# Odd mixer of a diffusion trunk: queries go to the scores without their norm, and each row's 1/rms scales its exponential and its maximum

## Chip, cores and metric

One core of one Trainium2 chip runs the whole program in one launch. The metric is the device time in microseconds (us). The kernel before was run three times: median 2787.94, from 2787.29 to 2793.31.

## What is computed

One step of a two-layer trunk on 640 tokens (512 latent "sample" tokens and 128 "prompt" tokens): FFN, mixer, FFN in each layer. Layer 0 has the even mixer (windowed attention and an mLSTM), layer 1 the odd one (HGRN2 and a dense attention whose queries and keys are normed). The change lies in the attention of the odd mixer:

```python
def _rms(x, g, eps=1e-6):
    return x * lax.rsqrt(jnp.mean(x * x, -1, keepdims=True) + eps) * g

dq = _rms(dq.reshape(bsz, L, D_KV, D_HEADS // D_KV, HEAD_DIM), q_norm)   # 2 key heads x 4 query heads, 64 wide
dk = _rms(dk.reshape(bsz, L, D_KV, HEAD_DIM), k_norm)
...                                               # sample: axial rotary on dq, dk; prompt: none
s = jnp.einsum('bqhgd,bkhd->bhgqk', q, k) * (q.shape[-1] ** -0.5)
p = jax.nn.softmax(s, axis=-1)                    # no mask, no sink
y = jnp.einsum('bhgqk,bkhd->bqhgd', p, v)
```

The sample's queries see 640 keys (its own 512 and 128 cached ones), the prompt's queries see the prompt's 128 keys. The new keys and values of the prompt are outputs too.

## The kernel before

Everything is kept in fp32. Each large product is made of three passes over operands split into a high and a low part (`mm3`), so a projection of 128 columns costs 24 matmuls for each half of the tokens. The tokens lie in five chunks of 128; the halves are tokens 0 to 383 and 384 to 639 (`HALVES`, `CHUNKS`), and the prompt is the last chunk. The framework schedules the program as a whole: it writes a fixed order for the queue of each engine (PE is TensorE, DVE VectorE, ACT ScalarE, POOL GpSimd, SP SyncE), and each engine takes its queue strictly in that order.

`odd` (L1204) begins with `proj_group`: the keys, the values, the first 128 columns of queries (two heads) and the first column block of HGRN head 0 are projected for half 1 and then for half 2. Keys and queries go through `normed` (L1223). For one half its `ev` does this: ACT copies the projection from PSUM (`q<-pj`; for half 2 in two pieces, since the prompt's chunk is kept apart), ACT squares it (`qsq`), PE multiplies the squares by `hsel` to get the mean square of each token and head (`qss`), DVE adds eps (`qrs`), and POOL raises to the power -0.5 (`qrp`, L1239). Then `rest` follows: PE transposes the 1/rms so that tokens lie along the free axis (`qrt`), ACT copies that out of PSUM (`rr`), PE multiplies it by `bsel` so that each partition of a head holds it (`qrb`), DVE forms q times gain times 1/rms (`q<-q,oc,qrb`, L133), and `rope` turns the sample's tokens (two DVE and two POOL operations, L624 to L632).

`queries(g)` in `odd` brings the second 128 columns of the first key group (g = 0), and both 128-column blocks of the second (g = 1); so four query projections in all, eight halves, go through `normed`, besides the key's two.

`attention` (L806) is a generator. For each key group g it copies and splits the keys and queries (`att_keys`, `q_stack`: `att<-kT`, `att<-q`) and then takes five blocks of 128 queries: four of the sample with five key tiles each (640 keys), and one of the prompt (j = 4) with one key tile. For each block `att_probs` (L694) makes the scores of four heads in PSUM (`s`; 384 and 256 columns, two matmuls each), their row maxima on DVE (`mx`), minus the maximum (`nm<-mx`, `minus`), the exponentials on ACT with `nm` as bias and the row sums as a second result (`pq<-s,nm` and `E<-s,nm`), and multiplies by the reciprocal of the sums on DVE. `att_out` (L774) then transposes the probabilities on PE (`pT`), splits them (`pr`, ACT and DVE), and multiplies them by the values (`pv`).

`weave` (L878) runs the attention beside the projections of the HGRN heads (`projections`, with the matmuls `pj` and `pn`): between the steps of the one, steps of the other are put, and the scheduler then places these matmuls, here called fillers, between the attention's own. What fillers the attention does not use are left to the three HGRN heads that follow, which are woven with the rest of the same projections.

Of the kernel before, what the change touches and what calls it, by code (L numbers as in the profile page):

```python
# [8 lines left out]
F32 = mybir.dt.float32  # L9
# [3 lines left out]
AF = mybir.ActivationFunctionType  # L13
ALU = mybir.AluOpType
# [3 lines left out]
P = 128  # L18
# [5 lines left out]
HALVES = ((0, 384), (384, 640))  # L24
HMAX = 384
CHUNKS = ((0, 1, 2), (3, 4))
# [23 lines left out]
class Net:  # L50
# [53 lines left out]

    def sm(self, n, tag):
        return self.small.tile([P, n], F32, tag=tag, name=tag)

# [585 lines left out]

    def att_probs(self, q, ks, tiles, masks, nsink, room, out):  # L694


        nc = self.nc
# [6 lines left out]
        def minus(c):  # L704
            if nsink is None:
                self.ts(nm[:, c], mx[:, c], -1.0, ALU.mult)
            else:
                self.stt(nm[:, c], mx[:, c], -1.0, nsink[:, c], ALU.mult, ALU.min)

        two = []  # L710
        if len(tiles) == 1:
            p = self.bank("a2", "s1")
# [4 lines left out]
            for hd in range(4):  # L717
                r = room[hd][0][:, 0:P]
                self.act(r, p[:, hd * P:(hd + 1) * P], AF.Exp, bias=nm[:, hd:hd + 1], accum_out=su[:, hd:hd + 1])
                out.append([r])  # L720
            yield
        else:
            for hd in range(4):
# [26 lines left out]
                for n, (p, r) in enumerate(parts):  # L750
                    self.act(r, p, AF.Exp, bias=nm[:, c], accum_out=su[:, 4 * n + hd:4 * n + hd + 1])
                if len(parts) > 1:
# [12 lines left out]
        for hd in range(4):  # L765
            n = len(tiles)
# [36 lines left out]
    def attention(self, kT, vv, queries, spec, yds, room, nsink=None):  # L803

        ar = Arena(self.xpool.tile([P, self.XN], F32R, tag="x", name="att"))
        st = ar.take(4 * NT).rearrange("p (a b) -> p a b", a=4)  # L806
        kk = ar.take(2 * 768).rearrange("p (a b) -> p a b", a=2)
        pr = self.wp.tile([P, 2, 2, 512], F32R, tag="w", name="pr")
        pr = [(pr[:, n, 0], pr[:, n, 1]) for n in range(2)]
        ks = kk[:, 0], kk[:, 1]  # L810
        qs = yield from queries(0)
        for n in range(10):
            g, j = divmod(n, 5)
            if j == 0:
                self.att_keys(kk, kT, g)
                for b in range(2):
                    self.q_stack(st[:, 2 * b:2 * b + 2], qs[b])
            tiles, masks = spec[j]
            probs = []
            yield from self.att_probs(st[:, :, j * P:(j + 1) * P], ks, tiles, masks,  # L820
                                      None if nsink is None else nsink[:, 4 * g:4 * g + 4], room, probs)
            if n == 4:
                qs = yield from queries(1)
            self.att_out(g, j, tiles, probs, vv, pr, yds[g])
# [64 lines left out]
    def even(self, mod, tail):  # L889
# [45 lines left out]
        def queries(g):  # L935
            qs = [[self.ft(e - a, "q") for a, e in HALVES] for _ in range(2)]
            for n, q in enumerate(qs):
                yield from self.proj_steps(w, (2 * g + n) * P, ev_rope(q), "v")
            return qs

# [166 lines left out]
    def mlstm_head(self, h, ins, temps, yb, in_v, ma, col, tri):  # L1107
# [8 lines left out]
        for hf, ch in enumerate(CHUNKS):  # L1116
# [3 lines left out]
            self.act(kn[:, ch[0]:ch[-1] + 1], ps[:, :len(ch) * P].rearrange("p (c t) -> p c t", t=P))  # L1120
        ws = self.sm(10, "ws").rearrange("p (a b) -> p a b", a=2)

# [81 lines left out]
    def odd(self, mod, tail):  # L1204
# [17 lines left out]
        def normed(c0, dst, which, pool=None):  # L1222
# [3 lines left out]
            def ev(hf, p):  # L1226
# [8 lines left out]
                for n in range(len(ch)):  # L1235
                    self.mm(pv[:, 2 * n:2 * n + 2], sq[:, n * P:(n + 1) * P], hsel)
                rs, rp = self.sm(6, "qrs"), self.sm(6, "qrp")
                self.ts(rs[:, :nch], pv[:, 0:nch], 1e-6, ALU.add)
                nc.gpsimd.tensor_tensor(out=rp[:, :nch], in0=rs[:, :nch], in1=self.mhalf[:, 0:nch], op=ALU.pow)  # L1239

                def rest():
# [7 lines left out]
                    for s, e, o in segs[hf]:  # L1249
# [5 lines left out]
            return self.col_unit(w, c0, pool), ev  # L1255

        q0 = [self.ft(e - a, "q") for a, e in HALVES]
        ya0, ya1 = (self.yt((2, NT), F32, "hi") for _ in range(2))
# [3 lines left out]
        self.proj_group([normed(3072, kT, 1, "v"), (self.col_unit(w, 3200, "v"), lambda hf, p: self.act(vT[hf], p)),  # L1262
                         normed(2560, q0, 0, "v")] + [(self.col_unit(w, c0), ev) for c0, ev in ahead])
        self.out_rows(kT[1][:, 256:384], self.o["new_cache_d_k"][0, 0].rearrange("t g d -> t (g d)"))
# [3 lines left out]
        def queries(g):  # L1268
            qs = [q0] if g == 0 else []
            new = [[self.ft(e - a, "q") for a, e in HALVES] for _ in range(len(qs), 2)]  # L1270
            late = []
            for n, q in enumerate(new):
                (wh, wl), ev = normed(2560 + (2 - len(new) + 2 * g + n) * P, q, 0, "v")
                for hf, (a, b) in enumerate(HALVES):
                    p = self.bank(("a1", "b")[hf], "pj")
                    self.mm3(p[:, :b - a], [(wh[:, k], wl[:, k], self.hh[:, k, a:b], self.hl[:, k, a:b]) for k in range(KD)])
                    late.append(ev(hf, p[:, :b - a]))
                    yield
                    if len(late) > 1:
                        late.pop(0)()  # L1280
            late.pop(0)()
            return qs + new

# [298 lines left out]
```

## Time and profile before

| | |
|---|---|
| median of three runs | 2787.94 us |
| the profiled execution, own time | 2790.35 us |
| its span (first to last instruction) | 2788.5 us |
| mean granted TensorE clock | 0.984 |
| busy: PE, DVE, ACT, POOL | 96%, 64%, 34%, 9% of the span |

The profiled execution is 2.41 us above the median; its span is 1.85 us short of its own time. Times in the profile count from the start of the span. A granted clock of 1.00 is the 2.4 GHz level of TensorE, 0.50 the 1.2 GHz one. The odd mixer's projections begin at about 1850 us, its attention runs from about 1915 to 2110 us, and HGRN heads 0 to 3 follow.

### The profile page before, as it was taken

To read this page: it belongs to the slowest core of one execution; us is meant where nothing else is said; L and a number is where in the kernel's file an instruction comes from. 1 tells how busy PE (TensorE), PEld (TensorE's weight loads), DVE (VectorE), ACT (ScalarE), POOL (GpSimd) and SP (SyncE) were. 2 spreads that over 40 slices of the span, in tenths; PEclk is the share of its full clock that TensorE was granted. 3 is DMA by queue.
4 is the path that set the end of the run, shared out by engine and by line. 5 is a ranking of instruction groups with operands and counts; after the bars stand their busy time and mean duration, and the time that the engine had idled before them with its cause. 6 is when DMAs were issued, how large, how long until landed. Compare 5 with 4: busy or idle time off the path is not lost.

```text
span 2788.5 us, 46663 instructions
## 1 busy us (share of the span) xinstructions
PE 2685.5 (96%) x19101; PEld 2577.2 (92%) x19101; DVE 1780.5 (64%) x3477; ACT 948.0 (34%) x1944; POOL 247.8 (9%) x282
## 2 busy tenths in 40 slices
PE   7999999999999999999999999998999899999998
PEld 4999999899888999999999999987798789999997
DVE  4967864676767976533896783375677788333334
ACT  3321221555554421311422122144555435112122
POOL 1000000410013000000300000042100022000003
PEclk9999999999999999999999999998999999999999
DMA  7554532221122544422264452221012224223111
GB/s 244 175 151 117 167 119 84 71 73 48 40 73 77 171 132 128 133 66 68 69 181 129 118 170 80 58 85 50 16 46 67 71 78 144 61 69 99 55 60 54
DMA packets 308195, 271.56 MB, mean 97 GB/s; under 512 B 13947, under 2 KB 257421, under 8 KB 307981
## 3 DMA queue, kind: packets, MB, share of 16 engines
q1 hardware_dynamic: 307620, 268.44, 32.5%
q8 instruction: 150, 2.46, 0.4%
q14 instruction: 65, 0.52, 0.1%
q10 hardware_dynamic: 360, 0.14, 0.0%
HBM read 259.36 MB, written 9.18 MB: 96 GB/s over the span
## 4 chain that ended last, share of the span: by engine, by line
PE 76%; DVE 11%; DMA 6%; ACT 3%; issue 2%; POOL 1%; SPq 0%; POOLq 0%; DVEq 0%; ACTq 0%
PE ps L136 36%; PE po L136 22%; PE pj L136 7%; DMA rawa<-in_ada_w 3%; PE pn L136 3%; DVE acc L133 2%; DMA raw<-in_ffn_w 2%; DVE w L126 1%; PE pv L136 1%; PE pT L139 1%; PE s L136 1%; DVE x L133 1%; DVE sum L126 1%; DVE h L126 1%; DVE x L126 1%
## 5 line engine op out<-in xcount | busy, mean ns | idle before, releaser
L136 PE MATMUL ps<-h,w 128*128 128x256 f32 (+1 forms) x7584 | 1124.0, 309 | 5.3 <-DVE h L126 2.7
L136 PEld LDWEIGHTS ps<-h,w 128*128 128x128 f32 x7584 | 1116.7, 190 | 8.1 <-DVE h L126 3.5
L136 PE MATMUL po<-g,wv 128*128 128x256 f32 (+1 forms) x4224 | 633.4, 310 | 9.8 <-DVE x L133 6.0
L136 PEld LDWEIGHTS po<-g,wv 128*128 128x128 f32 x4224 | 622.7, 189 | 17.7 <-DVE x L133 6.9
L133 DVE SCALAR_TENSOR_TENSOR x<-po,mod,x 128x128 f32<-128x128 f32 (+1 forms) x576 | 236.0, 435 | 276.8 <-PE po L136 275.4
L126 DVE TENSOR_TENSOR w<-raw,w 128x1024 fp32r<-128x1024 f32 x208 | 254.5, 1228 | 123.0 <-ACT w L123 122.1
L133 DVE SCALAR_TENSOR_TENSOR acc<-rawa,sc,acc 128x512 f32<-128x512 f32 x448 | 319.8, 757 | 11.2 <-DMA rawa<-in_ada_w 10.7
L123 ACT ACTIVATE wv<-raw 128x1024 fp32r<-128x1024 f32 x120 | 124.4, 1056 | 577.7 <-PE po L136 457.3
L123 ACT ACTIVATE w<-raw 128x1024 fp32r<-128x1024 f32 x208 | 218.6, 1056 | 160.2 <-issue 81.3
L500 POOL TENSOR_TENSOR ssq<-ssq,sq 128x384 f32<-128x384 f32 (+1 forms) x84 | 84.8, 1009 | 1716.9 <-ACT sq L123 1716.4
L123 ACT ACTIVATE g<-gt 128x384 fp32r<-128x384 f32 (+1 forms) x176 | 82.1, 466 | 397.7 <-DVE gt L126 397.5
L126 DVE TENSOR_TENSOR wv<-raw,wv 128x1024 fp32r<-128x1024 f32 x120 | 147.1, 1231 | 105.7 <-ACT wv L123 105.5
L126 DVE TENSOR_TENSOR gt<-sl,ps 128x384 f32<-128x384 f32 (+1 forms) x176 | 85.3, 484 | 184.3 <-PE ps L136 183.9
L136 PE MATMUL pj<-h,w 128*128 128x384 f32 (+1 forms) x864 | 150.0, 317 | 0.5 <-ACT mi L123 0.5
L123 ACT ACTIVATE sl<-ps 128x384 f32<-128x384 f32 (+1 forms) x176 | 75.9, 432 | 203.7 <-PE ps L136 203.6
L136 PE MATMUL ps<-h,wv 128*128 128x256 f32 (+1 forms) x864 | 140.4, 314 | 4.2 <-ACT h L123 2.5
L136 PE MATMUL pn<-w,h 128*128 128x256 f32 x960 | 140.2, 289 | 1.3 <-ACT mi L123 0.9
L136 PEld LDWEIGHTS ps<-h,wv 128*128 128x128 f32 x864 | 129.2, 191 | 7.5 <-ACT h L123 3.6
L136 PEld LDWEIGHTS pj<-h,w 128*128 128x128 f32 x864 | 132.0, 192 | 3.5 <-issue 1.2
L136 PEld LDWEIGHTS pn<-w,h 128*128 128x128 f32 x960 | 124.8, 191 | 4.3 <-ACT mi L123 1.1
L136 PE MATMUL pj<-h,wv 128*128 128x256 f32 (+1 forms) x672 | 117.1, 323 | 3.8 <-DVE t L126 1.8
L136 PEld LDWEIGHTS pj<-h,wv 128*128 128x128 f32 x672 | 103.5, 197 | 7.2 <-issue 2.1
(327 smaller groups left out, 2493.3 us busy)
## 6 DMA issues: line engine op xcount, KB each, us to landing
raw<-in_ffn_w SPq DMA_DIRECT2D x264, 512.0 KB
rawa<-in_ada_w SPq DMA_DIRECT2D x144, 512.0 KB
raw<-in_w_in_odd SPq DMA_DIRECT2D x18, 512.0 KB
raw<-in_w_in_even SPq DMA_DIRECT2D x14, 512.0 KB
raw<-in_w_in_even SPq DMA_DIRECT2D x16, 256.0 KB
raw<-in_w_out_even SPq DMA_DIRECT2D x8, 512.0 KB
raw<-in_w_in_odd SPq DMA_DIRECT2D x16, 256.0 KB
raw<-in_w_out_odd SPq DMA_DIRECT2D x8, 512.0 KB
```

The costliest lines, as they stand in the source:

```text
L123: return self.nc.scalar.activation(out=out, in_=in_, func=func, **k)
L126: return self.nc.vector.tensor_tensor(out=out, in0=in0, in1=in1, op=op)
L133: return self.nc.vector.scalar_tensor_tensor(out=out, in0=in0, scalar=s, in1=in1, op0=op0, op1=op1)
L136: return self.nc.tensor.matmul(out=out, lhsT=lhsT, rhs=rhs, start=start, stop=stop)
L139: self.nc.tensor.transpose(out, in_, self.ident[:in_.shape[0], :in_.shape[0]])
L500: nc.gpsimd.tensor_tensor(out=sums[1], in0=sums[1], in1=sq, op=ALU.add)
```

## The change

The four query projections have a function of their own, `query`. ACT copies the projection with the gain as its scale (`q<-pj,oc`, one instruction for each half), and `rope` follows at once. The squares, the mean squares and the power are as before, but the power's result is written into a tile `rq` with one column for each chunk and head, with tokens along the partitions, and that is all of the norm: no `qrt`, `rr`, `qrb`, and no product on DVE. The scores come out as 1/rms short of what they were. `att_probs` gets `rs`, the four columns of the block: `minus` is now a `scalar_tensor_tensor` that forms minus the maximum times 1/rms, and the exponential takes a pointer to 1/rms as its scale. The keys are normed as before. The small tiles `ws`, `qrs`, `qrp` have two buffers where they had four, and `rq` has two. The even mixer passes no `rs`; its instructions and their order are those of before, and so are the FFNs'.

```diff
-    def att_probs(self, q, ks, tiles, masks, nsink, room, out):
+    def att_probs(self, q, ks, tiles, masks, nsink, room, out, rs=None):
...
         def minus(c):
-            if nsink is None:
+            if rs is not None:
+                self.stt(nm[:, c], mx[:, c], -1.0, rs[:, c], ALU.mult, ALU.mult)
+            elif nsink is None:
                 self.ts(nm[:, c], mx[:, c], -1.0, ALU.mult)
...
+        scale = lambda hd: 1.0 if rs is None else rs[:, hd:hd + 1]
...
                 for n, (p, r) in enumerate(parts):
-                    self.act(r, p, AF.Exp, bias=nm[:, c], accum_out=su[:, 4 * n + hd:4 * n + hd + 1])
+                    self.act(r, p, AF.Exp, bias=nm[:, c], scale=scale(hd), accum_out=su[:, 4 * n + hd:4 * n + hd + 1])
...
+        def query(c0, dst, rq, b):
+            def ev(hf, p):
+                a, ch = HALVES[hf][0], CHUNKS[hf]
+                nch = 2 * len(ch)
+                self.act(dst[hf], p, scale=gq[:, 0:1])
+                sq = self.ft(HALVES[hf][1] - a, "qsq")
+                self.act(sq, p, AF.Square)
+                pv = self.bank("a2", "qss")
+                for n in range(len(ch)):
+                    self.mm(pv[:, 2 * n:2 * n + 2], sq[:, n * P:(n + 1) * P], hsel)
+                rs = self.sm(6, "qrs", 2)
+                self.ts(rs[:, :nch], pv[:, 0:nch], 1e-6, ALU.add)
+                two = lambda t: t[:, :nch].rearrange("p (c h) -> p c h", h=2)
+                nc.gpsimd.tensor_tensor(out=rq[:, ch[0]:ch[-1] + 1, 2 * b:2 * b + 2], in0=two(rs), in1=two(self.mhalf), op=ALU.pow)
+                n = 384 if hf == 0 else P
+                self.rope(dst[hf][:, :n], dst[hf][:, :n], a, n)
+            return self.col_unit(w, c0, "v"), ev
...
-                         normed(2560, q0, 0, "v")] + [(self.col_unit(w, c0), ev) for c0, ev in ahead])
+                         query(2560, q0, rq0, 0)] + [(self.col_unit(w, c0), ev) for c0, ev in ahead])
```

The change moves instructions on TensorE's queue. A row of its order is line, operation, out<-in, shape and count; `pj` are fillers (projections for HGRN).

The first place is `proj_group` at the end of the keys' and the first queries' half 1 and in half 2, on PE. Before:

```order
L136 MATMUL qss<-oc,qsq 128x2 x3
L136 MATMUL pj<-h,wv 128x256 x4
L139 MATMUL qrt<-ident,qrp 2x128 x3
L136 MATMUL pj<-h,wv 128x256 x11
L136 MATMUL qrb<-rr,oc 128x384
L136 MATMUL pj<-h,wv 128x256 x22
L136 MATMUL qss<-oc,qsq 128x2 x2
L136 MATMUL pj<-h,wv 128x256 x6
L139 MATMUL qrt<-ident,qrp 2x128 x2
L136 MATMUL pj<-h,wv 128x256 x4
L136 MATMUL qrb<-rr,oc 128x256
L136 MATMUL pj<-h,wv 128x256 x6
```

With the change:

```order
L136 MATMUL qss<-oc,qsq 128x2 x3
L136 MATMUL pj<-h,wv 128x256 x36
L136 MATMUL qss<-oc,qsq 128x2 x2
L136 MATMUL pj<-h,wv 128x256 x4
L139 MATMUL qrt<-ident,qrp 2x128 x2
L136 MATMUL pj<-h,wv 128x256 x7
L136 MATMUL qrb<-rr,oc 128x256
L136 MATMUL pj<-h,wv 128x256 x6
L136 MATMUL pj<-h,w 128x256 x14
L136 MATMUL qss<-oc,qsq 128x2 x2
```

The transposes and broadcasts that are left are those of the keys' second half; the four of the queries are gone, and the two `qss` of half 2 have moved against them.

The second place is the start of the attention on PE: the last scores of the first block's heads 0 and 1, heads 2 and 3 (`s` in the rows after the fillers), the next block's first scores, and the first transposes `pT`. Before:

```order
L136 MATMUL s_18951<-att 128x384 x2
L136 MATMUL pj<-h,wv 128x384 x3
L136 MATMUL s_18963<-att 128x384 x2
L136 MATMUL pj<-h,wv 128x384 x12
L136 MATMUL pj<-h,wv 128x256 x24
L136 MATMUL s_19007<-att 128x384 x2
L136 MATMUL s_19011<-att 128x256 x2
L136 MATMUL s_19019<-att 128x384 x2
L136 MATMUL s_19023<-att 128x256 x2
L136 MATMUL s_19121<-att 128x384 x2
L136 MATMUL s_19133<-att 128x384 x2
L139 MATMUL pT<-ident,pq 128x128 x8
```

With the change:

```order
L136 MATMUL s_18926<-att 128x256 x2
L136 MATMUL pj<-h,wv 128x384 x24
L136 MATMUL s_18966<-att 128x384 x2
L136 MATMUL s_18970<-att 128x256 x2
L136 MATMUL pj<-h,wv 128x256 x3
L136 MATMUL s_18978<-att 128x384 x2
L136 MATMUL pj<-h,wv 128x256
L136 MATMUL s_18982<-att 128x256 x2
L136 MATMUL pj<-h,wv 128x256 x20
L136 MATMUL s_19080<-att 128x384 x2
L136 MATMUL s_19092<-att 128x384 x2
L139 MATMUL pT<-ident,pq 128x128 x8
```

Before, 36 fillers follow the scores of heads 0 and 1, and none lies between the scores of head 2 and the transposes. Now 24 follow them, and 24 more lie between the scores of heads 2 and 3 and behind them; the transposes are still eight in a row.

The third place is the prompt's block of the first key group on PE (`s` 128x128), at which `queries(1)` begins (`qss`). Before:

```order
L136 MATMUL s_19531<-att 128x384 x2
L136 MATMUL s_19535<-att 128x256 x2
L136 MATMUL pj<-h,w 128x384
L136 MATMUL s_19606<-att 128x128 x8
L136 MATMUL qss<-oc,qsq 128x2 x3
L139 MATMUL pT<-ident,pq 128x128 x8
L136 MATMUL pv<-pr,vals 128x512
L136 MATMUL pj<-h,w 128x256 x6
L136 MATMUL pv<-pr,vals 64x512
L136 MATMUL pv<-pr,vals 128x512
```

With the change:

```order
L136 MATMUL pj<-h,w 128x256 x2
L136 MATMUL s_19494<-att 128x256 x2
L136 MATMUL pj<-h,w 128x256 x4
L136 MATMUL s_19565<-att 128x128 x8
L136 MATMUL qss<-oc,qsq 128x2 x3
L136 MATMUL pj<-h,w 128x256 x17
L139 MATMUL pT<-ident,pq 128x128 x2
L136 MATMUL pj<-h,w 128x256
L139 MATMUL pT<-ident,pq 128x128 x6
L136 MATMUL pj<-h,w 128x384 x4
L136 MATMUL pv<-pr,vals 128x512
L136 MATMUL pj<-h,w 128x384 x7
```

Before, no filler lies between the squares' matmul `qss`, the transposes and the first `pv`; now there are 17, 1 and 4.

## Rows read from the trace of the kernel before

**Rows 1.** The page, busy time of each engine over the whole span: us (share of the span) x instructions.

```profile
PE 2685.5 (96%) x19101; PEld 2577.2 (92%) x19101; DVE 1780.5 (64%) x3477; ACT 948.0 (34%) x1944; POOL 247.8 (9%) x282
```

**Rows 2.** What TensorE waited for, 1850 to 2080 us (the odd mixer from its key projection to the second block of the second key group): us in total, times, longest.

```profile
PE qrt L139 <- POOL qrp L1239: 4.5, 3, 2.5
PE s L136 <- ACT pq L123: 3.7, 5, 1.5
PE pT L139 <- DVE pq L130: 2.8, 2, 1.4
```

**Rows 3.** Timeline of TensorE where the first two query halves and the key's second half are normed: start us, us, engine, line, operation, out<-in, count [idle before <- what released it].

```profile
1879.36 0.49 PE L139 MATMUL qrt<-ident,qrp 128*2 128x128 f32 x3 [1.20 <-POOL qrp L1239]
1879.61 1.55 PE L136 MATMUL pj<-h,wv 128*128 128x256 f32 x11
1881.09 0.91 PE L136 MATMUL qrb<-rr,oc 2*128 2x384 f32 x2
1881.93 2.90 PE L136 MATMUL pj<-h,wv 128*128 128x256 f32 x22
...
1888.67 0.58 PE L139 MATMUL qrt<-ident,qrp 128*2 128x128 f32 x2 [2.55 <-POOL qrp L1239]
...
1897.85 0.38 PE L139 MATMUL qrt<-ident,qrp 128*2 128x128 f32 x2 [0.73 <-POOL qrp L1239]
1898.06 0.27 PE L139 MATMUL pm<-ident,kT 128*128 128x128 f32 x1
...
1898.80 0.69 PE L136 MATMUL qrb<-rr,oc 2*128 2x256 f32 x2
1899.42 5.13 PE L136 MATMUL pj<-h,wv 128*128 128x384 f32 x28
```

**Rows 4.** Timeline of TensorE at the start of the attention, same columns.

```profile
1920.87 5.13 PE L136 MATMUL pj<-h,wv 128*128 128x384 f32 x36
1927.53 2.25 PE L136 MATMUL s<-att 128*128 128x384 f32 x8 [1.53 <-ACT pq L123]
1931.11 2.03 PE L136 MATMUL s<-att 128*128 128x384 f32 x4 [1.34 <-ACT pq L123]
1934.53 2.46 PE L139 MATMUL pT<-ident,pq 128*128 128x128 f32 x8 [1.39 <-DVE pq L130]
1937.47 1.84 PE L136 MATMUL pv<-pr,vals 128*128 128x512 f32 x3 [0.47 <-ACT pr L123]
```

**Rows 5.** Stretches: start:end, us, busy time of PE, PEld, DVE, ACT, POOL with counts, granted TensorE clock (1.00 is 2.4 GHz, 0.50 is 1.2 GHz), DMA share, GB/s.

```profile
1930.00:1942.00 12.00, 9.01 (x28) 5.75 (x29) 9.00 (x22) 6.24 (x14) 0.00 (x0) 0.50 0.04 11
1994.00:2000.00 6.00, 5.42 (x20) 3.76 (x19) 4.96 (x15) 2.80 (x10) 0.00 (x0) 0.50 0.00 0
2050.00:2060.00 10.00, 10.00 (x78) 9.62 (x77) 7.06 (x25) 5.38 (x20) 0.00 (x0) 1.00 0.00 0
2186.00:2204.00 18.00, 12.16 (x257) 10.23 (x252) 17.33 (x24) 9.81 (x17) 0.00 (x0) 1.00 0.16 43
```

**Rows 6.** Timeline of ScalarE at the first exponentials of the attention.

```profile
1925.51 1.28 ACT L123 ACT_TABLE_LOAD   x1 [1.85 <-DVE mx L126]
1926.80 0.58 ACT L123 ACTIVATE pq<-s,nm 128x384 f32<-128x384 f32 x1
```

**Rows 7.** Timeline of TensorE at the prompt's block (j=4) at the end of the first key group, at one query chain of the second pair, and at the prompt's block that ends the second key group.

```profile
1989.27 1.04 PE L136 MATMUL s<-att 128*128 128x128 f32 x8
1991.44 0.83 PE L136 MATMUL qss<-oc,qsq 128*128 128x2 f32 x6 [1.14 <-ACT pq L123]
1993.71 2.46 PE L139 MATMUL pT<-ident,pq 128*128 128x128 f32 x8 [1.44 <-DVE pq L130]
1996.71 0.79 PE L136 MATMUL pv<-pr,vals 128*128 128x512 f32 x1 [0.53 <-ACT pr L123]
...
2015.02 0.69 PE L136 MATMUL qrb<-rr,oc 2*128 2x256 f32 x2 [0.50 <-ACT rr L123]
...
2094.92 0.41 PE L139 MATMUL pT<-ident,pq 128*128 128x128 f32 x2 [0.94 <-DVE pq L130]
```

**Rows 8.** Groups of instructions, shapes apart, 1850 to 2110 us, on ScalarE, VectorE and GpSimd: line, engine, operation, out<-in, shapes, count | busy us, mean ns | idle before.

```profile
L123 ACT ACTIVATE pq<-s,nm 128x384 f32<-128x384 f32 x32 | 18.6, 581 | 12.5 <-DVE nm L130 12.2
L123 ACT ACTIVATE E<-s,nm 128x256 f32<-128x256 f32 x32 | 15.1, 471 | 0.1
...
L123 ACT ACTIVATE rr<-qrt 2x384 f32<-2x384 f32 x5 | 2.4, 473 | 4.8 <-PE qrt L139 4.8
...
L130 DVE TENSOR_SCALAR nm<-mx 128x1 f32<-128x1 f32 x32 | 4.8, 151 | 0.7
...
L133 DVE SCALAR_TENSOR_TENSOR q<-q,oc,qrb 128x384 f32<-128x384 f32 x4 | 2.5, 615 | 2.5 <-PE qrb L136 2.4
...
L1239 POOL TENSOR_TENSOR qrp<-qrs,mhalf 128x6 f32<-128x6 f32 x5 | 8.1, 1613 | 80.9 <-DVE su L764 70.6 <-DVE qrs L130 8.3 <-DVE var L126 1.9
```

**Rows 9.** The same view on ScalarE, 600 to 920 us (the even mixer): forms with and without a pointer as scale.

```profile
L123 ACT ACTIVATE mi<-num,bden 128x128 f32<-128x128 f32 x20 | 6.2, 365 | 1.4 <-DVE bden L1175 1.2
...
L123 ACT ACTIVATE mi<-pn 128x128 f32<-128x128 f32 x17 | 4.7, 274 | 0.0
...
L123 ACT ACTIVATE mi<-pj 128x384 f32<-128x384 f32 x6 | 2.9, 490 | 6.0 <-PE pj L136 6.0
...
L123 ACT ACTIVATE yh<-ho,vec 128x384 f32<-128x384 f32 x4 | 2.2, 584 | 1.1 <-PE ho L139 1.1
```

More of the change, by code (lines that the diff above doesn't have):

```diff
@@ L103, in ft, with sm @@
         return self.fp.tile([P, self.FN], F32, tag="f", name=name)[:, :n]
-    def sm(self, n, tag):
-        return self.small.tile([P, n], F32, tag=tag, name=tag)
+    def sm(self, n, tag, bufs=4):
+        return self.small.tile([P, n], F32, tag=tag, name=tag, bufs=bufs)
     @staticmethod
@@ L718, in att_probs @@
                 r = room[hd][0][:, 0:P]
-                self.act(r, p[:, hd * P:(hd + 1) * P], AF.Exp, bias=nm[:, hd:hd + 1], accum_out=su[:, hd:hd + 1])
+                self.act(r, p[:, hd * P:(hd + 1) * P], AF.Exp, bias=nm[:, hd:hd + 1], scale=scale(hd),
+                         accum_out=su[:, hd:hd + 1])
                 out.append([r])
@@ L810, in attention @@
         ks = kk[:, 0], kk[:, 1]
-        qs = yield from queries(0)
+        qs, rq = yield from queries(0)
         for n in range(10):
@@ L820, in attention @@
             yield from self.att_probs(st[:, :, j * P:(j + 1) * P], ks, tiles, masks,
-                                      None if nsink is None else nsink[:, 4 * g:4 * g + 4], room, probs)
+                                      None if nsink is None else nsink[:, 4 * g:4 * g + 4], room, probs,
+                                      None if rq is None else rq[:, j])
             if n == 4:
-                qs = yield from queries(1)
+                qs, rq = yield from queries(1)
             self.att_out(g, j, tiles, probs, vv, pr, yds[g])
@@ L938, in queries @@
                 yield from self.proj_steps(w, (2 * g + n) * P, ev_rope(q), "v")
-            return qs
+            return qs, None
         spec = []
@@ L1120, in mlstm_head @@
             self.act(kn[:, ch[0]:ch[-1] + 1], ps[:, :len(ch) * P].rearrange("p (c t) -> p c t", t=P))
-        ws = self.sm(10, "ws").rearrange("p (a b) -> p a b", a=2)
+        ws = self.sm(10, "ws", 2).rearrange("p (a b) -> p a b", a=2)
         for hf, ch in enumerate(CHUNKS):
@@ L1236, in ev @@
                     self.mm(pv[:, 2 * n:2 * n + 2], sq[:, n * P:(n + 1) * P], hsel)
-                rs, rp = self.sm(6, "qrs"), self.sm(6, "qrp")
+                rs, rp = self.sm(6, "qrs", 2), self.sm(6, "qrp", 2)
                 self.ts(rs[:, :nch], pv[:, 0:nch], 1e-6, ALU.add)
@@ L1255, in normed @@
             return self.col_unit(w, c0, pool), ev
+        def query(c0, dst, rq, b):
[15 more added lines that the diff above has]
+            return self.col_unit(w, c0, "v"), ev
+        new_rq = lambda: self.small.tile([P, 20], F32, tag="rq", name="rq", bufs=2).rearrange("p (c h) -> p c h", c=5)
+        rq0 = new_rq()
         q0 = [self.ft(e - a, "q") for a, e in HALVES]
@@ L1268, in queries @@
         def queries(g):
[L1269 to L1273, printed above, removed]
+            qs, rq = ([], new_rq()) if g else ([q0], rq0)
+            while len(qs) < 2:
+                q = [self.ft(e - a, "q") for a, e in HALVES]
+                (wh, wl), ev = query(2560 + (2 * g + len(qs)) * P, q, rq, len(qs))
+                qs.append(q)
                 for hf, (a, b) in enumerate(HALVES):
@@ L1276, in queries @@
                     self.mm3(p[:, :b - a], [(wh[:, k], wl[:, k], self.hh[:, k, a:b], self.hl[:, k, a:b]) for k in range(KD)])
-                    late.append(ev(hf, p[:, :b - a]))
+                    ev(hf, p[:, :b - a])
                     yield
[L1279 to L1282, printed above, removed]
+            return qs, rq
         spec = [([0, 1, 2, 3, 4], None)] * 4 + [([5], None)]
```

## Prediction

> **What bounds the kernel now.** I read the busy times of the page first: TensorE is busy 96% of the span, the next engine 64% [rows 1]. So time falls only where TensorE loses work, waits less, or runs at its higher clock. The change touches nothing before 1850 us. I then listed TensorE's waits from 1850 to 2080 us: the three that the change can reach are the transposes of 1/rms waiting for POOL's power, 4.5 us in 3, the scores waiting for the exponentials that free their banks, 3.7 in 5, and the transposes of the probabilities waiting for the normalising product, 2.8 in 2 [rows 2]. The timeline shows where each lies [rows 3, 4, 7], and the granted clock of the stretches shows what they bring along: after the waits at the attention's start the clock is 0.50 (1.2 GHz) from 1930 to 1942 us, with 9.01 us of work in 12; after those at the prompt's block it is 0.50 from 1994 to 2000, with 5.42 in 6; in the steady part of the attention it is 1.00, with TensorE busy throughout [rows 5].
>
> **A. TensorE's own work.** A half that is normed costs TensorE two pieces: from its transposes to the next matmul, and from its broadcast to the next. For 384 tokens that is 1879.36 to 1879.61, 0.25, and 1881.09 to 1881.93, 0.84; for 256 tokens 1897.85 to 1898.06, 0.21, and 1898.80 to 1899.42, 0.62 [rows 3]. That is 1.92 for a projection; four projections lose it: **-7.7 us**. The squares and `qss` stay. This is work on the engine that sets the end, so nothing covers it.
>
> **B. Waits of those chains.** 1.20 and 0.73 for the power [rows 3] and 0.50 for `rr` [rows 7] go with what waited: 2.43. The key keeps its chain and its wait of 2.55 [rows 3]; in the new order the query's `qrt`, whose power stood ahead of the key's on POOL, is gone, so I expect some 2.0 there, but about as much comes back where `qss` and the next column block wait for their evacuations. I take **-2.2**, between 0 and -3.0.
>
> **C. Start of the attention.** Before, 36 fillers are spent behind the scores of heads 0 and 1, and then TensorE waits 1.53, 1.34, 1.39 and 0.47 [rows 4], 4.73 in all, and does 9.01 us of work at half clock, which at 2.4 GHz would take at least half of that: at most 4.5 more. Together some 9 us are lost. Now 48 fillers are spread: 24 behind the first scores, 24 between and behind those of heads 2 and 3. One filler takes 5.13/36 = 0.14. With maximum, `nm` and two exponentials (0.58 and 0.47 [rows 8]) the banks of the first head come free some 4 us after its scores, and TensorE arrives after six: no wait. The transposes still come eight in a row without a filler, so they still wait for four exponentials, sums and products, some 2 us, and the clock falls there as before. I put the loss left at 6.5: **-2.5**, between +1.5 (the fall of the clock comes to cover all of the block) and -9 (no wait is left).
>
> The table load in this chain takes 1.28 and the exponential starts 0.01 behind its end [rows 6]; it stands now ahead of the maxima, where it waits for nothing, and its move is part of C. The Trainium skill, page "ScalarE: Activation LUTs", section "What ACT_TABLE_LOAD costs", puts a drain of about 1.38 us behind each load, 2.66 in all. By it this move would give up to 1.38 more, C would be -3.9 and the time 1.4 lower; the row shows no such drain, and the sum goes by the row.
>
> **D. The prompt's block of the first group.** Before, `qss`, eight transposes and the first `pv` stand in a row without a filler and wait 1.14, 1.44 and 0.53 [rows 7], 3.1 in all; 5.42 us of work at half clock lose at most 2.7 more [rows 5]. Now 17 fillers (2.4 us at 0.14) stand behind `qss`, which covers the 1.44; 4 stand ahead of `pv`. The wait of `qss` for its bank stays in part. Of 5.8 I take **-3.5**, between +1 (the same fall of the clock, a little later) and -5.8.
>
> **E. The prompt's block of the second group.** The 0.94 in front of `pT` [rows 7] has 13 fillers before it where it had 3: **-0.9**, or 0.
>
> **F. Longer exponentials.** A pointer as scale is not in the attention of before. The nearest rows are the even mixer's: 365 against 274 for 128 columns, 584 against 490 for 384 [rows 9], 0.09 each. There are 72 exponentials (eight blocks of eight, two of four): 6.6 us more on ScalarE. It is busy 5.38 of 10 us in the steady part, where TensorE runs 10.00 of 10 [rows 5], so fillers cover it. ScalarE also loses eight `rr` (0.47 for the long ones [rows 8]). Where transposes follow without fillers (C, and partly D), a block's eight cost 0.7: **+1.0**, between 0 and all 6.6. `nm` takes a third operand; 0.15 as before [rows 8], nothing.
>
> **G. Fillers.** The order has 34 fewer matmuls of HGRN's projections between the first `qss` and the first of HGRN head 0 (24 of 256 columns, 10 of 384): 34 x 0.14 = 4.7 us. They come back under HGRN head 2, where 63 stand for 27. There TensorE is busy 12.16 of 18 us while VectorE is busy 17.33 [rows 5]: VectorE sets the pace and 5.8 us of TensorE are free. So HGRN starts 4.7 us earlier for the same total of TensorE's work. Whether the free time lies where the fillers are, the rows don't say: half, **-2.4**, between 0 (they are pure delay there) and -4.7.
>
> At nothing I put: VectorE's products (0.615 for a long half [rows 8]; VectorE waits for TensorE where they lie); POOL's power, which now releases `nm` as well (1.61 [rows 8]; in the queue it stands behind the first rope of its half, and the scores wait for that same rope); fewer small buffers (two halves are in flight); the one weight load that SP issues behind two cache loads, covered by the fillers ahead of the attention. If that cover is gone, each costs once 1 to 2 us at the first scores of a group.
>
> **Sum:** -7.7 - 2.2 - 2.5 - 3.5 - 0.9 + 1.0 - 2.4 = -18.2. The profiled execution took 2790.35, which is 2.41 above the median of the three runs; 2790.35 - 18.2 = 2772.1, and on the scale of the median **2770**.
>
> **Rivals.** *Only the work goes.* Each wait finds another event: the transposes of the probabilities wait as long as before, and the clock falls as often, merely at other places. Then A stands alone, -7.7 (with some of B -9): 2780, by 2777 to 2782. For it: both new orders keep transposes in a row; against it: 17 fillers where none were.
>
> *Both slow stretches vanish.* If C and D come to their ends (-9, -5.8) with A and B and E: -25.6, with G at its end -30: 2758 to 2762. For it: the steady part shows the pattern at clock 1.00 with fillers between transposes [rows 5]; against it: at C the transposes still have none.
>
> *HGRN takes it back.* VectorE sets the pace under heads 1 to 3 [rows 5]. If the 36 more fillers there stand in front of matmuls that VectorE waits for, they cost their 4.7, and with exponentials felt (F at 3) the sum is -7.7 - 2.2 + 4.7 + 3 = -2.2, with C, D and E at nothing: 2786, no change that can be told.
>
> *Slower.* The longer path from scores to probabilities decides: in each of the eight large blocks the eight exponentials run in sequence, and each is 0.09 longer, so the normalised probabilities come 0.74 later, while the fillers ahead of the transposes number the same. Where these don't reach, TensorE waits and its clock falls: a stretch like that of 1994 to 2000 loses up to 2.7 [rows 5]. A block then costs 3.4. From three such blocks on (10.2) it outweighs A and B; five give 17 - 9.9 = +7: 2795. For it: the transposes at 2094.92 already wait 0.94 [rows 7], so one place has no cover. Against it: no wait and full clock in the steady part [rows 5].
>
> *Not what it says.* The scheduler might hold all exponentials of a group until the last power of its second projection, since `rq` is one tile. The first block of each group would start 2 to 3 us later; it is in the range, at 2775.
>
> **How the numbers follow.** A measurement of this kernel can tell a change of about 0.2%, 5.6 us: faster is below 2782.4, slower above 2793.5. My forecast (2763 to 2777) has 0.48; only the work 0.20; both stretches vanish 0.14; HGRN takes it back 0.12; slower 0.06. The first three are faster, 0.82; the fourth is no change, 0.12. All terms at their low ends give -31, at their high ends +1.4, neither likely; the range from 2756 to 2784 takes in the first three cases with their bounds and leaves out most of the last two.
>
> **What would show it.** Right for A and B: no `qrt` or `qrb` but the key's (two of each, one of each half), and the waits of `qrt` for POOL at one, near 2. For C: the scores of heads 2 and 3 start without a wait, while a wait stays in front of the first transposes with a clock near 0.5 behind it. For D: clock 1.00 through the prompt's block and transposes without a wait. For F: exponentials of 0.67 and 0.56. For G: TensorE busier in the stretch under HGRN head 2, with the same span. It would be wrong if new waits for the exponentials stood inside the steady blocks, or if the attention ended 20 us sooner and the whole run only 8.

## The result and the profile after

The changed kernel takes 2765.48 us (median of 5, 2763.53 to 2766.95) where the kernel before takes 2789.81 (median of 5, 2787.29 to 2793.31): ratio 0.9917, 95% interval 0.9907 to 0.9928. That is 24.3 us less; the forecast was 18.2. Its profiled execution took 2766.95, span 2765.2. The page, as [rows 1]:

```profile
PE 2673.9 (97%) x19065; PEld 2571.5 (93%) x19065; DVE 1778.2 (64%) x3465; ACT 951.3 (34%) x1932; POOL 246.3 (9%) x282
```

What TensorE waited for, 1850 to 2080 us, as [rows 2]:

```profile
PE pT L139 <- DVE pq L130: 4.0, 9, 1.7
PE s L136 <- ACT pq L123: 1.6, 2, 1.2
PE qss L136 <- ACT qsq L123: 1.6, 2, 1.2
...
PE qrt L139 <- POOL qrp L1245: 0.8, 1, 0.8
```

One wait for a power is left, the key's, 0.8, where the key and the queries had three with 4.5; the scores' waits fell from 3.7 to 1.6; those of the transposes rose from 2.8 to 4.0, and `qss` now waits 1.6 for the squares. The places on TensorE: the key's second half, as [rows 3],

```profile
1872.18 0.72 PE L136 MATMUL qss<-oc,qsq 128*128 128x2 f32 x6
1872.77 4.54 PE L136 MATMUL pj<-h,wv 128*128 128x256 f32 x36
1877.29 0.61 PE L136 MATMUL qss<-oc,qsq 128*128 128x2 f32 x4
...
1879.25 0.38 PE L139 MATMUL qrt<-ident,qrp 128*2 128x128 f32 x2 [0.77 <-POOL qrp L1245]
```

the attention's start, as [rows 4],

```profile
1903.95 4.36 PE L136 MATMUL pj<-h,wv 128*128 128x384 f32 x24
1908.14 0.74 PE L136 MATMUL s<-att 128*128 128x384 f32 x4
...
1913.09 0.62 PE L136 MATMUL s<-att 128*128 128x384 f32 x2 [0.40 <-ACT pq L123]
1915.42 0.44 PE L139 MATMUL pT<-ident,pq 128*128 128x128 f32 x2 [1.71 <-DVE pq L130]
...
1918.21 1.84 PE L136 MATMUL pv<-pr,vals 128*128 128x512 f32 x3 [0.48 <-ACT pr L123]
```

and the first prompt's block, as [rows 7]:

```profile
1975.73 0.83 PE L136 MATMUL qss<-oc,qsq 128*128 128x2 f32 x6 [0.67 <-ACT pq L123]
1976.42 2.27 PE L136 MATMUL pj<-h,w 128*128 128x256 f32 x17
1978.53 0.38 PE L139 MATMUL pT<-ident,pq 128*128 128x128 f32 x2
...
1981.47 0.97 PE L136 MATMUL pj<-h,w 128*128 128x384 f32 x4 [0.84 <-DVE hi L133]
1982.28 0.39 PE L136 MATMUL pv<-pr,vals 128*128 128x512 f32 x1
```

Heads 2 and 3 (1908.14) start without a wait, `pT` still waits at the start (1.71), and at the prompt's block fillers stand where three waits were; 0.67 is left in front of `qss`, two of 0.15 between the transposes, and there is a new one of 0.84 in front of the fillers ahead of the first `pv`. The exponentials have the forecast length (0.67 and 0.56), and the table load stands ahead of the maximum:

```profile
L123 ACT ACTIVATE pq<-s,nm,rq 128x384 f32<-128x384 f32 x32 | 21.4, 670 | 9.0 <-DVE nm L133 8.6
L123 ACT ACTIVATE E<-s,nm,rq 128x256 f32<-128x256 f32 x32 | 17.9, 560 | 0.1
```

```profile
1903.36 1.28 ACT L123 ACT_TABLE_LOAD   x1
1905.62 0.67 ACT L123 ACTIVATE pq<-s,nm,rq 128x384 f32<-128x384 f32 x1 [0.98 <-DVE nm L133]
```

The load ends 0.98 before the exponential, which waits for `nm`. That is less than the drain of which the prediction speaks, so here too, as in [rows 6], the rows show none. The pointer costs 89 ns (581 to 670, 471 to 560, [rows 8]). The Trainium skill, page "ScalarE: Activation LUTs", section "What ACT_TABLE_LOAD costs", gives about 93 ns for each pointer operand; the rows agree within 4.

**Where the time went.** Five stretches of the kernel before and of the changed one, cut at the same instructions of TensorE (first `qss`, transposes of the prompt's keys, first `pv`, first `qss` of the second group, first `lv` of HGRN head 0, first `lv` of head 3); columns as [rows 5]. Before:

```profile
1857.00:1898.00 41.00, 36.49 (x207) 32.94 (x207) 23.19 (x57) 17.31 (x45) 19.05 (x19) 0.83 0.25 75
1898.00:1937.50 39.50, 34.69 (x203) 28.84 (x201) 21.18 (x65) 17.90 (x51) 6.85 (x9) 0.89 0.16 47
1937.50:1991.40 53.90, 52.24 (x326) 46.36 (x326) 37.20 (x99) 30.92 (x85) 0.00 (x0) 0.95 0.14 40
1991.40:2101.60 110.20, 105.86 (x689) 93.19 (x690) 78.62 (x213) 61.61 (x162) 11.13 (x12) 0.97 0.12 34
2101.60:2223.90 122.30, 105.83 (x1639) 93.92 (x1638) 90.30 (x153) 60.35 (x150) 4.56 (x6) 0.99 0.23 69
```

After:

```profile
1853.90:1885.10 31.20, 30.39 (x200) 28.37 (x200) 20.82 (x58) 16.37 (x42) 16.72 (x20) 0.95 0.32 99
1885.10:1918.20 33.10, 29.17 (x191) 26.67 (x190) 19.81 (x59) 18.73 (x48) 8.08 (x9) 0.99 0.20 54
1918.20:1975.70 57.50, 54.27 (x332) 47.44 (x332) 40.77 (x104) 33.83 (x87) 2.23 (x2) 0.95 0.13 38
1975.70:2073.20 97.50, 94.37 (x631) 84.23 (x631) 74.25 (x201) 61.69 (x159) 8.71 (x10) 1.00 0.12 34
2073.20:2198.60 125.40, 114.94 (x1678) 103.11 (x1676) 92.98 (x154) 60.40 (x145) 4.54 (x6) 0.93 0.23 70
```

The first column behind the colon gives the lengths: 41.0, 39.5, 53.9, 110.2 and 122.3 became 31.2, 33.1, 57.5, 97.5 and 125.4, 22.2 less in all. Length less PE busy is idle time: 31.8 us before, 21.6 after. Work and clock make up the rest: in the first stretch a mean clock of 0.83 over 41 us says that (1 - 0.83)/0.5 x 41 = 14 us ran at 1.2 GHz, after 3. In front of these stretches, where the order is the same, the profiled executions differ by 3.1 us; that is no effect of the change (in the profiles of the experiments the first `qss` starts between 1851.7 and 1858.6, whichever the kernel).

### The profile page after: what moved, and what is told of

It reads as the page before. It is cut to its first block, busy times and chain, and to the rows that moved or that the text cites. A ratio compares the mean times of both kernels' runs of the same rounds, so it can differ in the third digit from the quotient of the medians.

```text
span 2765.2 us, 46542 instructions
## 1 busy us (share of the span) xinstructions
PE 2673.9 (97%) x19065; PEld 2571.5 (93%) x19065; DVE 1778.2 (64%) x3465; ACT 951.3 (34%) x1932; POOL 246.3 (9%) x282
## 5 line engine op out<-in xcount | busy, mean ns | idle before, releaser
L126 DVE TENSOR_TENSOR w<-raw,w 128x1024 fp32r<-128x1024 f32 x208 | 254.4, 1228 | 121.8 <-ACT w L123 121.2
```

Source lines behind the costliest of these rows:

```text
L126: return self.nc.vector.tensor_tensor(out=out, in0=in0, in1=in1, op=op)
```

## The experiments

Each was timed in five rounds beside the kernel before on its chip, except where said; a difference is in medians of one session, and the interval of a ratio is about ±0.0013, 3.6 us.

**The changed kernel again, and the kernel before again** (no edit).

> The changed kernel once more, unaltered, for a second profile. Theory (work, waits and clock): the 22 us won in the odd mixer are 7.7 of removed TensorE work, about 10 of TensorE's waits and the rest fewer stretches at half clock; what is lost again later (4 us under HGRN head 3, 2 at the start of the FFN behind the mixer) are two falls of the clock at waits that the kernel before has too. If these falls hang on chance of the execution, this profile has them at other places and the account of work and waits repeats within 1 us; time 2760 to 2767. Rival (the program sets them): both falls come again at the same instructions, clock near 0.5 over the same scan steps of HGRN head 3 and at the first mean of the FFN.

> The kernel before, unaltered, for a second profile: the falls of the clock at the key's wait, at the attention's start and at the prompt's block come again at the same instructions (theory: each stands behind waits of over 1 us in a row without fillers), those under HGRN head 3 and at the FFN's start may or may not. Rival: the falls at the three places move or vanish as well, and with them the 4 to 7 us that the account gives to the clock.

The changed kernel: 2763.11 against 2786.26, ratio 0.9923 (0.9909 to 0.9936). In its profile (span 2757.2) the first four stretches repeat within 0.6 us, but the last took 121.2, and the first mean of the FFN kept its clock. Here are the second profile's rows (HGRN, FFN), then the first one's FFN:

```profile
2070.60:2191.80 121.20, 109.65 (x1673) 98.39 (x1672) 92.66 (x154) 60.10 (x145) 4.55 (x6) 0.99 0.23 69
...
2249.00:2258.00 9.00, 7.52 (x60) 6.92 (x59) 7.20 (x21) 1.15 (x3) 2.92 (x3) 1.00 0.19 60
```

```profile
2256.00:2266.00 10.00, 8.92 (x49) 8.72 (x50) 6.44 (x19) 0.97 (x3) 2.03 (x3) 0.66 0.14 54
```

Same order, another clock: 0.66 or 1.00 at the FFN, 0.93 [the last row of the stretches after] or 0.99 under HGRN. These falls differ between executions of one program; under HGRN alone they make 4.2 us. The kernel before again (one execution, 2790.24): its clock fell at the key, the attention's start and the prompt's block as in the first profile, each at the same instructions, and so did the two other falls, just behind the first `qss` and under HGRN head 3. Profiles of other runs that share this order up to the key differ, though: behind the first `qss` the clock is low for 3.4 us in three of them (the run with the scale alone, the one with more fillers and the one with the second group alone) where it was 6.8, and in the last of these the fall at the key came one wait sooner, behind the 1.20 of [rows 3]. So the three places hang on the program; the exact instruction and the length do not always. Both theories hold in the main.

**Work put back, waits not.**

```diff
                 self.rope(dst[hf][:, :n], dst[hf][:, :n], a, n)
+                m = HALVES[hf][1] - a
+                pt = self.bank("a2", "qrt")
+                for n in range(len(ch)):
+                    self.tr(pt[0:2, n * P:(n + 1) * P], self.mhalf[:, 2 * n:2 * n + 2])
+                pb = self.bank("a2", "qrb")
+                self.mm(pb[:, :m], bsel, self.cossin[0:2, 0, 0:m])
```

> The changed kernel with the removed TensorE work put back as work that nothing waits for: in each of the eight query halves the transposes and the broadcast matmul run on constants into a bank that nobody reads. Theory (term A is on the path): +7.7 against the changed kernel, 2773. Rival (TensorE has room for it, and only the waits counted): within 2 us of the changed kernel, 2766.

2770.56, 7.5 above the changed kernel of that session (2763.11), known to some ±5: term A, -7.7, is on the path. Its profile agrees: the first four stretches take 6.0 more than those of the changed kernel, with 13 fewer fillers (1.8) in them, so 7.8.

**One part at a time.** The second group old (for the second group alone new the same stands under `g == 0`, and the first projection is `normed` again), and the first projection alone new:

```diff
         def queries(g):
+            if g == 1:
...
+                    (wh, wl), ev = normed(2560 + (2 - len(new) + 2 * g + n) * P, q, 0, "v")
...
+                return new, None
```

```diff
+        nc.vector.memset(rq0[:, :, 2:4], 1.0)
...
-                         normed(2560, q0, 0, "v")] ...
+                         query(2560, q0, rq0, 0)] ...
```

> The changed kernel with the second key group's queries normed as before (two of the four query projections; their exponentials take no pointer), the first group's as changed. The stretch from the prompt's block of group 0 to the first scores of group 1 was 11.4 us shorter after the change, with 22 fewer fillers in it (3.1 us): theory: about 8 us come back, 2774 (3.8 of work, the rest waits and half clock). Rival (the gain sits in the first group alone, in the key's chain and the attention's start): 3.8 or less, 2769 or below.

> The other half of the run before: the second group's two query projections as changed, the first group's normed as before. If the parts add up, this one gains what undoing it cost, -7.3 against the kernel before. Rival (the parts share one gain, through the fillers or the clock): clearly less than 7.3, near the 3.8 of work alone.

> The kernel before with only the first of the four query projections as changed (the one that is projected together with the key); the other three are normed as before, and their two columns of the first group's 1/rms hold ones; the result is the reference's. Theory: this one projection carries more than its work of 1.9, since the key's power no longer stands behind a query's on GpSimd: the key's wait falls from 2.55 to 0.8, two waits go, and the clock no longer falls behind them: about -8 against the kernel before. Rival (term B as predicted): its work and its own two waits, -3.9.

With the second group old: 2770.44, 7.3 come back. Second group alone: 2779.52 against 2786.64, -7.1 (ratio 0.9975, 0.9965 to 0.9985). In time the parts add up. The first projection alone: 2776.02 against 2786.64, -10.6 (0.9965, 0.9953 to 0.9978; -6.1 to -13.1): over 40% of the gain by its median. By difference some 6 are left for the first group's second projection, with an uncertainty as large.

But none of these edits is one part alone: for each kernel the scheduler writes a new order, and with it the number of fillers changes that the attention leaves to HGRN. Counted from first `lv` of HGRN head 0 to first `lv` of head 3, with the length of that stretch and its granted clock:

| kernel | fillers `pj` | us | clock |
|---|---|---|---|
| before | 144 | 122.3 | 0.99 |
| changed, first and second profile | 178 | 125.4 and 121.2 | 0.93 and 0.99 |
| second group old | 173 | 124.6 | 0.95 |
| second group alone | 219 | 126.1 | 0.99 |
| first projection alone | 173 | 123.7 | 0.96 |
| scale alone (below) | 172 | 123.5 | 0.96 |
| no scale (below) | 226 | 129.5 | 0.97 |

So the run with the first projection alone also holds 29 fewer fillers ahead of HGRN, 4.1 us at 0.14. If HGRN takes these for nothing, the rival comes to 3.9 + 4.1 = 8.0, which lies within the interval: the time does not refute it. The first stretch does, which holds the same 161 fillers in both. It is shown for the first projection alone and for the kernel before with more fillers under HGRN, whose order here is that of before:

```profile
1852.90:1883.30 30.40, 29.12 (x199) 26.99 (x200) 20.78 (x58) 16.38 (x42) 16.78 (x20) 1.00 0.33 101
```

```profile
1854.00:1893.40 39.40, 34.90 (x208) 31.36 (x208) 23.17 (x57) 17.32 (x45) 19.09 (x19) 0.87 0.25 77
```

9.0 less, of which 0.8 to 1.6 is an early fall of the clock (3.4 us, behind the first `qss`) that only the second has (with and without 3.4 us of it this stretch took 41.0 and 39.4 before the change, 31.2 and 30.4 after it); 7 to 8 stay, twice the rival's 3.9, which is my term B with its work.

**Longer exponentials alone, and left out.**

```diff
-                self.ts(nm[:, c], mx[:, c], -1.0, ALU.mult)
+                self.stt(nm[:, c], mx[:, c], -1.0, self.one4[:, c], ALU.mult, ALU.mult)
...
+                    self.act(r, p, AF.Exp, bias=nm[:, c], scale=1.0 if nsink is not None else self.one4[:, c],
```

> The kernel before with one part of the change alone: minus the maximum and every exponential of the odd attention take a pointer to a column of ones, the queries are normed as before, the result is the reference's. Term F of the prediction: +1.0, between 0 and +6.6, so about 2790.8 where the kernel before takes 2789.8. Theory after the result: +1 to +3, with new waits of the probabilities' transposes for the normalising product in the steady blocks. Rival (the pointer's 6.6 us on ScalarE are fully felt): 2796.

```diff
-        scale = lambda hd: 1.0 if rs is None else rs[:, hd:hd + 1]
+        scale = lambda hd: 1.0
```

> The changed kernel without its additions in the attention: the exponentials have an immediate scale of one and minus the maximum has no third operand; the 1/rms is still computed but enters nothing, so the queries' norm is left out of the result. Theory (term F is near nothing, as in the run with the scale alone): 0 to -2 against the changed kernel, 2761 to 2763. Rival (the new waits of the transposes in the second and third block, 2.8 us in the profile, come from the longer exponentials): -3 to -5.

Alone on the kernel before: 2783.95 against 2786.26, ratio 0.9993 (0.9984 to 1.0002); the 6.6 us on ScalarE are not fully felt. Left out of the changed kernel: 2765.84, ratio 0.9918 (0.9905 to 0.9932), like the changed kernel. Neither time is the price of the longer exponentials alone. The first order leaves HGRN 28 fillers more (3.9 us), which can hide a cost; the second leaves it 48 more, and in it the clock falls at the prompt's block again (6.8 us), as before the change. What the profiles show is local: with the same fillers as before, the third stretch (four blocks with the longer exponentials) takes 54.3 with the scale alone, where it took 53.9, and 54.4 with the second group old:

```profile
1918.00:1972.40 54.40, 53.18 (x327) 46.49 (x327) 37.01 (x98) 32.46 (x85) 0.00 (x0) 0.95 0.14 40
```

So the longer exponentials cost some 0.4 there. They are not what makes this stretch 57.5 in the changed kernel, with waits of 1.1 for the product and 1.2 for the exponentials. In the order without the scale, too, `pT` waits 4.6 us in all for the product.

**More fillers under HGRN.**

```diff
+        def more():
+            for _ in range(4):
+                dm = self.bank("a1", "dm")
+                for _ in range(9):
+                    self.mm(dm[:, :256], self.hh[:, 0, :P], self.hh[:, 0, P:3 * P])
+                yield
...
+            self.weave(head(Arena(xt), n), *([(more(), 1)] if n == 2 else []), (islice(proj, 2 * 3 + 5), 1))
```

> The kernel before with 36 more matmuls of 256 columns that nothing needs (36 x 0.14 = 5.0 us), woven into HGRN head 2. Theory on term G: from HGRN head 0 to head 3 VectorE sets the pace, the stretch takes 121 to 122 us with 144 or 178 filler matmuls `pj` in it, so they cost nothing to 1 us: 2787. Rival (term G's other end, TensorE sets the pace there too): +5, 2791.

> The changed kernel with the same 36 matmuls at the same place. Theory: the 34 fillers that the change left to HGRN have used most of the free time (178 took 121 us in one profile, 219 in the run with group 1 alone took 126), so these are felt: +3 to +5, 2767 where the changed kernel takes 2763. Rival (the free time is far from used up): 0 to +1.

Before: 2786.82 against 2787.80, ratio 0.9998 (0.9989 to 1.0007): free, or 2 us at most. After: 2764.34, ratio 0.9915 (0.9901 to 0.9929): in the medians nothing is felt there either, but the difference between this ratio and the changed kernel's 0.9917 and 0.9923 is known to some 4 us only, so the 3 that I expected at the least are not ruled out. The stretch from HGRN head 0 to 3, of the one and the other:

```profile
2097.00:2220.90 123.90, 111.87 (x1675) 99.34 (x1674) 90.78 (x153) 60.66 (x150) 4.56 (x6) 0.97 0.23 71
```

```profile
2077.30:2201.50 124.20, 114.49 (x1709) 103.04 (x1708) 92.51 (x154) 60.31 (x145) 4.54 (x6) 0.99 0.23 72
```

TensorE is 6 us busier than before without the 36 in the first (111.87 for 105.83), and its idle time shrank by 4.4. The second, at the same clock of 0.99 as the second profile of the changed kernel, takes 124.2 where that took 121.2: in the profile some 3 of the 5 us are felt. With still more fillers, 219 and 226, the stretch takes 126.1 and 129.5 (table above): the free time has an end.

**The attention's start kept busy.**

```diff
+            if rq is not None and n == 0:
+                dm = self.pm("dm")
+                for _ in range(14):
+                    self.mm(dm[:, :256], kk[:, 0, :P], kk[:, 0, P:3 * P])
```

```diff
-        self.weave((self.attention(kT, vv, queries, spec, yds, room), 1), (islice(proj, 2 * 2 + 5), 1))
+        self.weave((islice(proj, 2 * 2 + 5), 1), (self.attention(kT, vv, queries, spec, yds, room), 1))
```

> The changed kernel with 14 more matmuls of 256 columns (some 2 us at full clock) that nothing needs, put by the order ahead of the next block's first scores at the attention's start, where TensorE waits 0.4 and 1.7. Theory: the waits take them in, and if these waits are what lets the clock fall (6.8 us at half clock in every profile of the changed kernel), the fall goes and up to 3 us are won: 2760 where the changed kernel takes 2763. Rival (the fall comes from the transposes that follow at VectorE's pace, or the matmuls only delay them): no change to +2.

> The changed kernel with the two woven generators exchanged, so that the projections are a step ahead of the attention; nothing else. In its order the first block's transposes have fillers between them (14, 3, 3, 3) where they had none. Theory: the waits of 0.4 and 1.7 and the 6.8 us at half clock at the attention's start go, worth up to 5 us: 2758 to 2761. Rival: the fillers are then missing at the two prompt's blocks, which wait and lose their clock as they did before the change: no gain, or +2.

The clock at the first transposes: the changed kernel, then with 14 matmuls more, then with the projections first (and its stretch under HGRN):

```profile
1915.00:1924.00 9.00, 7.64 (x29) 5.56 (x30) 7.43 (x14) 4.17 (x6) 0.00 (x0) 0.63 0.20 60
```

```profile
1917.00:1924.00 7.00, 5.61 (x31) 3.56 (x31) 6.90 (x16) 3.95 (x6) 0.00 (x0) 1.00 0.01 2
```

```profile
1915.00:1924.00 9.00, 9.00 (x67) 8.27 (x67) 6.06 (x19) 4.32 (x14) 0.00 (x0) 1.00 0.01 2
2072.30:2194.10 121.80, 108.52 (x1644) 97.05 (x1644) 91.23 (x151) 59.87 (x144) 4.54 (x6) 0.94 0.21 65
```

Both do what they were meant to do at their place: the clock is 1.00 there. But 2763.02 (0.9917, 0.9904 to 0.9931) and 2762.44 (0.9914, 0.9901 to 0.9928) are the changed kernel's time. For the second the rows say why: what the attention wins in fillers HGRN lacks, and HGRN takes its 122 us with fewer of them too (145). Its rival came in part: ahead of the first prompt's block there is a wait of 1.5 for `hi` on VectorE and 3.4 us at half clock behind it. For the first a gain of up to 3 us is within the interval, and its profile shows one in place: the second and third stretch, with 14 matmuls more in them, take 87.7 at a clock of 1.00,

```profile
1888.00:1975.70 87.70, 82.16 (x537) 73.52 (x534) 60.18 (x161) 52.38 (x134) 10.22 (x11) 1.00 0.16 45
```

where the changed kernel's two profiles have 90.6 and 90.1. So the waits ahead of the first transposes bring the fall there along, as the theory says. HGRN's stretch in that execution took 125.7 at 0.93, which hides the gain; whether it shows in the mean of many runs stays open. No version here beats the changed kernel by more than can be measured.

## Why the prediction was right, and where its sizes were wrong

**A, TensorE's work (-7.7): right**; 7.5 came back with the work, within some ±5.

**B, the chains' waits (-2.2): mis-sized, about -6, and for a wrong reason.** The first stretch is 9.8 shorter, of which A gives 1.9 and an earlier, shorter fall of the clock (chance: the kernel before with the scale alone and with more fillers under HGRN, in the same order there, has it short too) 1.6. I took only 0.5 off the key's wait of 2.55, because a query's power "stood ahead of the key's on POOL". The rows say otherwise. VectorE and GpSimd of the kernel before, then of the changed one:

```profile
1884.09 2.32 DVE L126 TENSOR_TENSOR att<-kT,att 64x384 fp32r<-64x384 f32 x2 [0.27 <-ACT att L123]
1886.44 0.16 DVE L130 TENSOR_SCALAR qrs<-qss 128x4 f32<-128x4 f32 x1
1886.52 1.22 DVE L126 TENSOR_TENSOR wv<-raw,wv 128x1024 fp32r<-128x1024 f32 x1
```

```profile
1884.79 1.21 POOL L632 TENSOR_TENSOR q<-t,t 128x384 f32<-128x384 f32 x1
1886.68 1.93 POOL L1239 TENSOR_TENSOR qrp<-qrs,mhalf 128x4 f32<-128x4 f32 x1 [0.69 <-DVE qrs L130]
```

```profile
1877.93 0.16 DVE L130 TENSOR_SCALAR qrs<-qss 128x4 f32<-128x4 f32 x1 [3.22 <-PE qss L136]
1878.21 1.24 DVE L126 TENSOR_TENSOR wv<-raw,wv 128x1024 fp32r<-128x1024 f32 x1
```

```profile
1878.18 1.02 POOL L1245 TENSOR_TENSOR qrp<-qrs,mhalf 128x4 f32<-128x4 f32 x1 [1.34 <-DVE qrs L130]
```

GpSimd stood idle for 0.69 and waited for `qrs`, and that stood behind two `att<-kT` on VectorE (2.32 us), 1.1 after `qss` had ended. Now `qrs` follows `qss` at once, and the power takes 1.02 for 1.93; the wait is 0.77. With it the fall of the clock behind it (1888 to 1895, which I had in the profile and did not count) is gone: worth some 3 us. It is gone in the run with the first projection alone too, whose key also waits 0.8. That the place behind `att<-kT` is the cause was read, not tried apart. The power's length has a pattern in the rows: before, it began while VectorE already ran the weight split `wv<-raw,wv` and ended 0.87 after that (1888.61 and 1887.74); now it begins 0.03 ahead of one. In the fourteen profiles all eleven powers of 128x4 that begin under such a split end 0.87 to 0.88 after it and take 1.93 to 2.05; the 33 that begin while VectorE runs nothing take 1.01 to 1.02.

**C and F (-2.5 and +1.0): right in sum, by luck.** From the prompt's key transposes to the second group's `qss` the two stretches are 2.8 shorter with six more fillers (0.8) in them; less A's 1.9 that leaves -1.7 where -1.5 was forecast. Taken apart, the second stretch is 6.4 shorter, 4.5 of it beyond A, almost twice C, and the third is 3.6 longer with 0.8 of fillers: 2.8 of new cost in the blocks that I had called steady, a sign that I had named for being wrong. It is not F, which costs some 0.4 there: with the second group old the exponentials of these blocks are as long and the third stretch takes 54.4. The order that the scheduler wrote makes it; which of its moves does was not tried.

**D, E and the rest of B (-4.9): about -3.3.** The fourth stretch is 12.7 shorter with 40 fewer fillers (5.6) and 3.8 of A, which leaves -3.3. The clock stays up through the prompt's block (mean 1.00 for 0.97). With the second group old it falls there again, for 6.8 us.

**G, the fillers (-2.4): mis-sized, up to -4.7.** I halved it because the rows did not say whether the free time lies where the fillers are. It does: on the kernel before 36 more cost nothing, and with the 34 more of the change HGRN takes 121.2 at the clock of before (122.3). In the first profile it gives 3 us back (125.4), in the one with the 14 matmuls too (125.7), both at a clock of 0.93. Whether its clock falls there more often than that of the kernel before (0.99 in both profiles) is not shown; if it does, G is nearer to my -2.4.

These terms, read off the stretches of the profiles, give -7.7 - 6 - 1.7 - 3.3 - 4.7 = -23.4, beside -24.3 and -23.2 of the two sessions. The path, work and waits of TensorE with the clock behind them, held; the reason for the key's wait and the steady blocks did not. The sum was 5 to 6 short through B (3.8) and G (up to 2.3), less 1.6 that D, E and the rest of B had too much. The rivals *Only the work goes* (2777 to 2782), *HGRN takes it back* (2786) and *Slower* (2795) fall with the time itself, 2765.5 and 2763.1. *Both slow stretches vanish* (2758 to 2762) came nearest in time, but not in its mechanism: the prompt's block keeps its clock, the attention's start loses it still (0.63, behind a wait of 1.71). *Not what it says* did not come: the first exponential starts at 1905.62, and the last power of its group ended at 1902.3, ahead of its scores.

## What to carry to other kernels

On an engine that sets the end, count a removed instruction twice: its own time, and the wait and clock fall that it or its chain brings; two thirds of the gain here were not work. Before a wait is put down to a queue, read what that queue's engine was idle for just ahead. Work moved into a stretch that another engine paces is free until its idle time is used up (at like clocks HGRN with 178 fillers took as long as with 144, with 219 and 226 it took 4 and 7 us more), and work taken out of such a stretch gives nothing. Where a scheduler writes the whole order anew, no edit is one part alone: compare stretch by stretch, with the moved work counted, before a part is given its time.

## What had not been expected of the hardware

The same program with the same waits is granted 2.4 GHz in one execution and 1.2 GHz in the next, at some places (0.66 or 1.00 over ten microseconds at the FFN's start), while at others the fall came in every profile: 4 of 4 with the key's old wait of 2.55 (a fifth in that order fell one wait sooner, and its key waited 1.45), 4 of 4 at the attention's start in the changed kernel's order. Two profiles of one program so differ by 8 us of span (2765.2 and 2757.2), a third of the change.
